# Attention slopes without scaled distance tables, weight splits moved from GpSimd to VectorE, keys made head by head, in a hybrid transformer block

## The chip, the cores and the metric

The kernel runs on one core of a Trainium2 chip. A core has TensorE (PE, matrix products, results in eight PSUM banks), VectorE (DVE), ScalarE (ACT), GpSimd (POOL) and SyncE (SP, which here issues nearly all transfers). The metric is the device time of one execution in microseconds; lower is better.

## The reference

One layer on 512 tokens of width 1024, in float32:

```
h = rms_norm(x); q, k, v, u = split(h @ w_in)          # 4 x 512 columns
a = attention(q, k, v)                                 # 8 heads x 64, causal
    score[t, s] = q[t].k[s] / 8 - slope_h * (t - s);  slope_h = 2 ** -(h + 1), h = 0..7
p = pool(u)       # 4 groups x 128: (trailing mean over 16, 8, 4 or 2 tokens - token) @ w_pool[g] * scale
x = x + concat(a, p) @ w_out
x = x + relu(rms_norm(x) @ w_up) ** 2 @ w_down         # 4096 wide
out = rms_norm(x)
```

The block-sparse selection of the reference takes every past block at this length, so the attention is plain causal attention with a linear distance penalty.

## The kernel before, in words

Every float32 product is made of three matmuls: each factor is split into a high part that PE takes as it is and a low remainder, and `mm3` (lines 193 to 195) adds high x high, high x low and low x high. A split is a cast on ACT and a subtraction, on VectorE or GpSimd, that waits for it (`split_into`, lines 144 and 145). Weights come by DMA into three `raw` buffers (`load`); `prefetch` splits the oldest into `whi` and `wlo` and issues the load of the chunk three further on. The subtraction's engine is the argument `sub`.

The instructions of each engine run in the order in which the program writes them; `in_program_order` fixes that. A stage that is written earlier on one engine therefore holds up what is written behind it on that engine, however ready that is.

The span falls into: normalisation and values (to about 37 us); q0, k0 and u3, the projections of the first pair of heads and of one pooling group; three rounds of the loop at line 554; the output projection in 128-token tiles (`out_tile`), first with the pooling half of w_out, then with the attention half; and the feed-forward part, which is most of the span and which the change doesn't touch.

The heads go in four pairs. A round i of the loop (I call the rounds by the pair whose values they attend: first, second, third pair) does, in program order:

- `pool_mix(g)`: on VectorE the pooled mean minus the token (L505) and a correction of its first 16 columns, where fewer tokens are there to average (L507, L508); then the splits of the mean and of w_pool;
- the projection q of the next pair and its scaled split (`queries`, L387 on ACT, L388 on VectorE), and one weight split;
- the projection u of the next group (`pool_sum`: a copy on ACT, running sums on GpSimd, L498), and two distance tables (`tables`, L369, on GpSimd): the table of token distances `dist`, times the slope of each head;
- `turn`: the probabilities of the pair before are transposed on PE (L455) and split (L459, L461);
- two weight splits; in the third round both have the subtraction on GpSimd;
- the projection k of the next pair and `keys`: for each of two heads, two tiles ka and kb of 128 partitions hold the high half, from ACT, and the low half, from VectorE, in opposite order. Scores take ka first, then kb. Both heads lie in one PSUM bank, on different partitions; where both ACT and VectorE read the bank, the program orders the reads by waits;
- in the third round, between the splits and `keys`, `pool_mix(0)` as well;
- `attend` of the pair (16 matmuls, L473); its result is copied and subtracted (L477 and L478 on ACT, L479 on VectorE, into `cl`), `pool_out` (three matmuls; L519 on ACT, L520 on VectorE), a second `pool_out` and one more weight split in the third round;
- `softmax` of the next pair: 16 score matmuls (L426), for each head in three groups of one bank each, then for each of 8 pieces a minimum with a sum on VectorE (L432: scores, which are negated, plus table, and the smallest), the exponential on ACT (L434) and the scaling on VectorE (L414).

PSUM tiles all come from one rotation of eight banks (`bank`): a new tile waits until the tile eight allocations back has been read.

```
    PART = ((slice(0, 64), slice(64, 128)), (slice(64, 128), slice(0, 64)))
    GROUPS = ((0, 2), (1,), (3,))
```

## Time and profile before

| | |
|---|---|
| runs of before, median of 3 (lowest, highest) | 529.42 us (529.0, 530.33) |
| profiled execution, its own time | 529.51 us |
| its span, first to last instruction | 527.7 us |
| mean granted clock of PE (1 = 2.4 GHz) | 0.992 |
| PE busy | 514.7 us (98%) |
| VectorE busy | 378.9 us (72%) |
| ScalarE busy | 247.8 us (47%) |
| GpSimd busy | 56.0 us (11%) |

Busy shares are means over the whole span. A matmul's duration on the page is longer than its distance to the next one, as matmuls overlap, so a busy PE can hide a lower rate; the granted clock of a stretch and the distance of starts show that. A wait is put down to the instruction that ended last before the waiting one started.

### The profile page before, as it was taken

Reading aid. Unit: us, or ns where it says so; the run is one execution under the profiler, and the core shown is the slowest. Engines: PE = TensorE matmul, PEld = TensorE weight load, DVE = VectorE, ACT = ScalarE, POOL = GpSimd, SP = SyncE. Lnnn points to the kernel's source line nnn. Section 1 sums busy time; section 2 is a strip of 40 time slices with the busy share of each in tenths; the row PEclk is TensorE's granted clock in tenths of the full one; section 3 lists DMA queues with packets and bytes.
Section 4 is the critical chain, followed back from the end, with each engine's and each line's share of the span. In section 5 each row is a group of like instructions: output and inputs, shape, how many; then the busy total and the mean of one; then the engine's idle time right before and its main releaser. Section 6 shows DMA issues by size and latency. Waiting matters only on the chain.

```text
span 527.7 us, 6731 instructions
## 1 busy us (share of the span) xinstructions
PE 514.7 (98%) x2411; PEld 429.4 (81%) x2411; DVE 378.9 (72%) x619; ACT 247.8 (47%) x415; POOL 56.0 (11%) x59
## 2 busy tenths in 40 slices
PE   8999999998999999999999999999999998999995
PEld 5888878886888899888888888888888886888884
DVE  5764898889986756777756777577776778977363
ACT  5534586866744333423323233345655555456033
POOL 2330342516300100000000000000000000000002
PEclk9999999999799999999999999999999999999999
DMA  8441141303224208697777897785688754683012
GB/s 293 146 119 42 49 125 37 126 1 125 81 81 126 74 0 279 202 292 261 260 255 253 251 308 269 250 276 183 218 291 306 273 199 159 223 287 128 0 52 111
DMA packets 74053, 92.48 MB, mean 175 GB/s; under 512 B 4257, under 2 KB 49825, under 8 KB 74018
## 3 DMA queue, kind: packets, MB, share of 16 engines
q1 hardware_dynamic: 73440, 90.98, 52.0%
q10 hardware_dynamic: 578, 1.05, 0.5%
q8 instruction: 19, 0.31, 0.2%
q14 instruction: 16, 0.13, 0.1%
HBM read 75.24 MB, written 16.78 MB: 174 GB/s over the span
## 4 chain that ended last, share of the span: by engine, by line
PE 88%; DVE 6%; ACT 2%; issue 2%; DMA 1%; POOL 0%; SPq 0%; POOLq 0%
PE bank L193 26%; PE bank L195 26%; PE bank L194 26%; PE bank L293 5%; PE bank L426 2%; PE bank L215 1%; DMA wvr<-in_w_in_dram 1%; PE bank L455 1%; DVE ptl L461 1%; DVE p L432 1%; ACT whi L144 1%; DVE wlo L145 1%; DVE ka L398 1%; DVE mx L508 0%; PE bank L473 0%
## 5 line engine op out<-in xcount | busy, mean ns | idle before, releaser
L193 PE MATMUL bank<-hh,whi 128*128 128x512 f32 (+1 forms) x376 | 141.8, 377 | 0.2 <-DVE qs L388 0.2
L195 PE MATMUL bank<-hh,wlo 128*128 128x512 f32 (+1 forms) x376 | 141.4, 376 | 0.0
L194 PE MATMUL bank<-hl,whi 128*128 128x512 f32 (+1 forms) x376 | 141.4, 376 | 0.0
L145 DVE TENSOR_TENSOR wlo<-raw,whi 128x1024 fp32r<-128x1024 f32 x87 | 107.5, 1238 | 27.5 <-ACT whi L144 25.4
L144 ACT CAST whi<-raw 128x1024 fp32r<-128x1024 f32 x90 | 94.1, 1054 | 31.1 <-PE bank L195 23.5
L193 PEld LDWEIGHTS bank<-hh,whi 128*128 128x128 f32 x376 | 70.8, 188 | 13.1 <-PE bank L455 0.4
L195 PEld LDWEIGHTS bank<-hh,wlo 128*128 128x128 f32 x376 | 70.8, 188 | 12.8
L194 PEld LDWEIGHTS bank<-hl,whi 128*128 128x128 f32 x376 | 70.8, 188 | 12.7
L193 PE MATMUL bank<-whi,ah 128*128 128x512 f32 x168 | 65.5, 390 | 0.7 <-DVE a L846 0.7
L194 PE MATMUL bank<-wlo,ah 128*128 128x512 f32 x168 | 65.4, 390 | 0.0
L195 PE MATMUL bank<-whi,al 128*128 128x512 f32 x168 | 65.4, 390 | 0.0
L208 POOL TENSOR_TENSOR rstd<-ms,mhalf 128x1 f32<-128x1 f32 x12 | 6.6, 552 | 388.4 <-DVE ms L203 388.4
L717 DVE TENSOR_TENSOR a<-bank,z 128x512 f32<-128x512 f32 (+1 forms) x31 | 19.7, 636 | 34.2 <-ACT z L711 34.2
L711 ACT ACTIVATE z<-bank 128x512 f32<-128x512 f32 (+1 forms) x35 | 19.6, 560 | 48.9 <-PE bank L195 46.6
L144 ACT CAST ah<-a 128x1024 fp32r<-128x1024 f32 (+1 forms) x28 | 26.3, 941 | 27.9 <-issue 17.8
L145 DVE TENSOR_TENSOR al<-a,ah 128x1024 fp32r<-128x1024 f32 (+1 forms) x28 | 30.5, 1088 | 11.0 <-ACT ah L144 11.0
L193 PEld LDWEIGHTS bank<-whi,ah 128*128 128x128 f32 x168 | 31.5, 188 | 7.6 <-DVE a L846 1.1
L194 PEld LDWEIGHTS bank<-wlo,ah 128*128 128x128 f32 x168 | 31.6, 188 | 6.5
L195 PEld LDWEIGHTS bank<-whi,al 128*128 128x128 f32 x168 | 31.6, 188 | 6.5
L144 ACT CAST rl<-rh 128x512 fp32r<-128x512 f32 x14 | 8.7, 622 | 57.6 <-DVE rh L684 57.6
L199 ACT ACTIVATE sq<-x 128x512 f32<-128x512 f32 (+2 forms) x17 | 10.3, 606 | 33.0 <-DVE x L886 19.6
L434 ACT ACTIVATE p<-p,mn 128x128 f32<-128x128 f32 (+3 forms) x32 | 18.0, 562 | 11.5 <-DVE rs L413 5.8
(149 smaller groups left out, 774.2 us busy)
## 6 DMA issues: line engine op xcount, KB each, us to landing
raw<-in_w_up_dram SPq DMA_DIRECT2D x32, 512.0 KB, 6.3
raw<-in_w_down_dram SPq DMA_DIRECT2D x18, 512.0 KB, 3.3
rh<-in_w_down_dram SPq DMA_DIRECT2D x14, 512.0 KB, 3.3
ta<-rh SPq DMA_DIRECT2D x14, 512.0 KB, 7.3
tb<-rl SPq DMA_DIRECT2D x14, 512.0 KB, 6.6
raw<-in_w_down_dram SPq DMA_DIRECT2D x28, 256.0 KB, 3.4
raw<-in_w_in_dram SPq DMA_DIRECT2D x12, 512.0 KB, 3.8
raw<-in_w_out_dram SPq DMA_DIRECT2D x8, 512.0 KB, 3.2
```

What stands on the lines that cost most here:

```text
L144: nc.scalar.copy(hi, src)
L145: (sub or nc.vector).tensor_sub(lo, src, as32(hi))
L193: nc.tensor.matmul(acc, lhsT=a[0], rhs=b[0], start=first, stop=False)
L194: nc.tensor.matmul(acc, lhsT=a[0], rhs=b[1], start=False, stop=False)
L195: nc.tensor.matmul(acc, lhsT=a[1], rhs=b[0], start=False, stop=last)
L199: nc.scalar.activation(dump, src, AF.Square, scale=1.0 / 32, accum_out=ss[:, k:k + 1])
L208: nc.gpsimd.tensor_tensor(rstd, ms, mhalf, op=ALU.pow)
L293: nc.tensor.matmul(acc, lhsT=a, rhs=w, start=n == 0 and kd == 0, stop=n == 2 and kd == KD - 1)
L426: nc.tensor.matmul(by_qi[qi], lhsT=qs[:, tok(qi)], rhs=k[:, :w], start=n == 0, stop=n == 1)
L434: nc.scalar.activation(p[:, :w], p[:, :w], AF.Exp, scale=-1.0, bias=mn, accum_out=sm)
L711: nc.scalar.activation(z[:, :n * HT], acc, AF.Relu)
L717: nc.vector.tensor_mul(a_p[f // 2][:, at_slots, :], halves(acc), halves(z[:, :n * HT]))
```

## The change

The distance tables are gone. The penalty's slope goes in two places instead: `queries` scales by -0.125 / slope, and the minimum adds the one table `dist` to the scores and multiplies the sum by the slope (`scale` of the same instruction, 1.0 before). `keys` makes both tiles of a head before it begins the next head. All weight subtractions are on VectorE: `cast_next` writes the cast on ACT, and returns a function that writes the subtraction and the next load later. In the first two rounds the first subtraction stands ahead of the keys, as before, and the second behind them; in the third, the first stands inside `pool_mix(0)` between the correction and the splits of the mean, the second behind the keys, and the third, as before, behind the pooling products.

```
+    def cast_next():
+        raw, shape = raws.pop(0)
+        hi = wp.tile([P] + shape, F32R, tag="whi", name="whi")
+        lo = wp.tile([P] + shape, F32R, tag="wlo", name="wlo")
+        nc.scalar.copy(hi, raw)
+        ready.append((hi, lo))
+        def rest():
+            nc.vector.tensor_sub(lo, raw, as32(hi))
+            load()
+        return rest
...
-    def tables(i):
-        tabs = []
-        for j in range(2):
-            tabs.append(at.tile([P, T], F32, tag="tab", name="tab"))
-            nc.gpsimd.tensor_scalar_mul(tabs[j], dist, 2.0 ** (-8.0 * (2 * i + j + 1) / NH))
-        return tabs
...
+    def slope(h):
+        return 2.0 ** (-8.0 * (h + 1) / NH)
...
-    def queries(acc):
+    def queries(acc, i):
         heads = []
-        for m, o in PART:
+        for j, (m, o) in enumerate(PART):
+            scale = -0.125 / slope(2 * i + j)
             qs = at.tile([P, T], F32R, tag="qs", name="qs")
-            nc.scalar.activation(qs[m], acc[m], AF.Copy, scale=-0.125)
-            nc.vector.scalar_tensor_tensor(qs[o], acc[m], -0.125, as32(qs[m]), op0=ALU.mult, op1=ALU.subtract)
+            nc.scalar.activation(qs[m], acc[m], AF.Copy, scale=scale)
+            nc.vector.scalar_tensor_tensor(qs[o], acc[m], scale, as32(qs[m]), op0=ALU.mult, op1=ALU.subtract)
...
         for j, (m, o) in enumerate(PART):
-            heads[j] += [at.tile([P, T], F32R, tag=k, name=k) for k in ("ka", "kb")]
-            nc.scalar.copy(heads[j][1][m], acc[m])
-        for j, (m, o) in enumerate(PART):
-            ka, kb = heads[j][1:]
+            ka, kb = [at.tile([P, T], F32R, tag=k, name=k) for k in ("ka", "kb")]
+            heads[j] += [ka, kb]
+            nc.scalar.copy(ka[m], acc[m])
+            nc.scalar.copy(kb[o], as32(ka[m]))
             nc.vector.tensor_sub(ka[o], acc[m], as32(ka[m]))
-            nc.scalar.copy(kb[o], as32(ka[m]))
-        for j, (m, o) in enumerate(PART):
-            ka, kb = heads[j][1:]
             nc.vector.tensor_copy(kb[m], as32(ka[o]))
...
-                    nc.vector.tensor_tensor_reduce(out=p[:, :w], in0=by_qi[qi], in1=tabs[j][:, T - w:], scale=1.0,
+                    nc.vector.tensor_tensor_reduce(out=p[:, :w], in0=by_qi[qi], in1=dist[:, T - w:],
+                                                   scale=slope(2 * i + j),
                                                    scalar=BIG, op0=ALU.add, op1=ALU.min, accum_out=mn)
...
-    def pool_mix(g, u, s, wpl):
+    def pool_mix(g, u, s, wpl, between=None):
...
+        if between is not None:
+            between()
         split_into(*m_s, mx[:, PAD:])
         split_into(*w_s, wpl)
...
         sums = pool_sum(g - 1, acc)
-        tabs = tables(i + 1)
         pt = [turn(p) for p in probs]
-        prefetch(1, nc.vector if i < NPAIR - 2 else nc.gpsimd)
+        rests = [cast_next(), cast_next()]
         acc = project()
         if i < NPAIR - 2:
-            prefetch(1)
+            rests[0]()
         else:
-            prefetch(1, nc.gpsimd)
-            before, mean = mean, pool_mix(0, *sums)
+            before, mean = mean, pool_mix(0, *sums, rests[0])
         keys(heads, acc)
+        rests[1]()
         fixes = [attend(2 * i + j, pt[j]) for j in range(2)]
         pool_out(g, *(mean if i < NPAIR - 2 else before))
         if i == NPAIR - 2:
             pool_out(0, *mean)
-            prefetch(1, nc.gpsimd)
+            prefetch(1)
```

ScalarE in the first pair's round, from the last weight cast to the copies of the attended values (ka and kb are the key tiles, ch and fix parts of the attended values; the brackets name the engines whose signals an instruction waits for). Before:

```order
L144 CAST whi<-raw 128x1024 [waits DMAHW4_49]
L395 CAST ka<-bank 64x512 [waits PE_49]
L395 CAST ka<-bank 64x512
L399 CAST kb<-ka 64x512 [waits Activation_49] x2
L477 CAST ch_141<-bank 64x512 [waits PE_49]
L478 COPY fix<-bank 64x512
L477 CAST ch_141<-bank 64x512 [waits PE_49]
L478 COPY fix<-bank 64x512
```

In the change, whose lines stand 9 to 19 further down:

```order
L163 CAST whi<-raw 128x1024 [waits DMAHW4_49]
L408 CAST ka<-bank 64x512 [waits PE_49]
L409 CAST kb<-ka 64x512 [waits Activation_49]
L408 CAST ka<-bank 64x512 [waits DVE_49]
L409 CAST kb<-ka 64x512 [waits Activation_49]
L487 CAST ch_141<-bank 64x512 [waits PE_49]
L488 COPY fix<-bank 64x512
L487 CAST ch_141<-bank 64x512 [waits PE_49]
L488 COPY fix<-bank 64x512
```

The first head's second tile now comes ahead of the second head's first tile, and that one has gained a wait for VectorE.

VectorE in the third pair's round, from the end of the pooled mean (mx) to the first minimum of the next softmax (mxl and wpll are the low parts of the mean and of w_pool, wlo the low part of a weight chunk, cl that of the attended and pooled values). Before:

```order
L508 TENSOR_TENSOR mx<-mx,u 128x16 [waits DVE_49]
L145 TENSOR_TENSOR mxl<-mx,mxh 128x512 [waits Activation_49]
L145 TENSOR_TENSOR wpll<-wpl,wplh 128x128 [waits DMAHW6_49,Activation_49]
L398 TENSOR_TENSOR ka<-bank,ka 64x512 [waits PE_49,Activation_49]
L398 TENSOR_TENSOR ka<-bank,ka 64x512
L402 CAST kb<-ka 64x512 [waits DVE_49] x2
L479 TENSOR_TENSOR cl_151<-bank,ch_143 64x512 [waits PE_49,Activation_49] x2
L520 SCALAR_TENSOR_TENSOR cl_154<-bank,psc,ch_146 128x512 [waits Activation_49]
L520 SCALAR_TENSOR_TENSOR cl_153<-bank,psc,ch_145 128x512 [waits Activation_49]
L432 ISA p,mn<-bank,tab 128x128 [waits PE_49,Pool_49]
```

In the change, from behind the correction of mx to just ahead of that minimum:

```order
L167 TENSOR_TENSOR wlo<-raw,whi 128x1024 [waits DMAHW3_49,Activation_49]
L145 TENSOR_TENSOR mxl<-mx,mxh 128x512 [waits Activation_49]
L145 TENSOR_TENSOR wpll<-wpl,wplh 128x128 [waits DMAHW6_49,Activation_49]
L410 TENSOR_TENSOR ka<-bank,ka 64x512 [waits Activation_49]
L411 CAST kb<-ka 64x512 [waits DVE_49]
L410 TENSOR_TENSOR ka<-bank,ka 64x512 [waits Activation_49]
L411 CAST kb<-ka 64x512 [waits DVE_49]
L167 TENSOR_TENSOR wlo<-raw,whi 128x1024 [waits DMAHW4_49]
L489 TENSOR_TENSOR cl_151<-bank,ch_143 64x512 [waits PE_49,Activation_49] x2
L532 SCALAR_TENSOR_TENSOR cl_154<-bank,psc,ch_146 128x512 [waits Activation_49]
L532 SCALAR_TENSOR_TENSOR cl_153<-bank,psc,ch_145 128x512 [waits Activation_49]
L145 TENSOR_TENSOR wlo<-raw,whi 128x1024 [waits DMAHW5_49,Activation_49]
```

Three subtractions wlo have come in, one ahead of mxl, one between the keys and cl, and one ahead of the minimum; the second head's ka waits for ACT anew, and the minimum (no longer shown) waits for PE alone.

## Rows read from the trace of the kernel before

**Rows 1.** The page: busy time of PE, and its slices (40 to the span).

```profile
PE 514.7 (98%) x2411; PEld 429.4 (81%) x2411; DVE 378.9 (72%) x619; ACT 247.8 (47%) x415; POOL 56.0 (11%) x59
...
PE   8999999998999999999999999999999998999995
```

**Rows 2.** Windows: stretch, then busy us (instructions) of each engine, PEclk, DMA share, GB/s.

```profile
99.94:105.78 5.84, 5.84 (x37) 5.22 (x35) 4.47 (x8) 5.32 (x9) 1.91 (x2) 1.00 0.52 182
124.36:136.88 12.52, 9.72 (x40) 7.86 (x39) 10.64 (x17) 8.12 (x16) 4.70 (x3) 0.75 0.24 85
```

**Rows 3.** Waits of PE: line, releaser, us in total, times, longest.

```profile
PE bank L193 <- ACT wplh L144: 1.6, 1, 1.6
PE bank L426 <- DVE kb L402: 1.5, 2, 0.8
...
PE bank L193 <- DVE qs L388: 0.2, 1, 0.2
```

**Rows 4.** Timeline of PE, first pair's scores: start us, us, line, operation.

```profile
77.77 0.22 PE L426 MATMUL bank<-ka,qs 128*128 128x128 f32 x1
78.82 0.30 PE L426 MATMUL bank<-kb,qs 128*128 128x128 f32 x1 [0.83 <-DVE kb L402]
...
81.35 0.40 PE L193 MATMUL bank<-hh,whi 128*128 128x512 f32 x1
```

**Rows 5.** Timeline of PE, third pair: second score matmul, first output-tile matmul.

```profile
132.26 0.45 PE L426 MATMUL bank<-kb,qs 128*128 128x128 f32 x1 [0.68 <-DVE kb L402]
...
136.88 0.63 PE L193 MATMUL bank<-whi,ch 128*128 128x512 f32 x1
```

**Rows 6.** Timeline of VectorE, second pair: correction of the pooled mean.

```profile
89.14 0.17 DVE L507 TENSOR_TENSOR mx<-us,rc 128x16 f32<-128x16 f32 x1
```

**Rows 7.** Timeline of VectorE, third pair: the pooled mean and its split.

```profile
123.05 0.68 DVE L505 SCALAR_TENSOR_TENSOR mx<-us,u 128x512 f32<-128x512 f32 x1
123.65 2.42 DVE L507 TENSOR_TENSOR mx<-us,rc 128x16 f32<-128x16 f32 x1
126.11 2.29 DVE L508 TENSOR_TENSOR mx<-mx,u 128x16 f32<-128x16 f32 x1
129.08 0.69 DVE L145 TENSOR_TENSOR mxl<-mx,mxh 128x512 fp32r<-128x512 f32 x1 [0.68 <-ACT mxh L144]
```

**Rows 8.** Timeline of GpSimd, third pair.

```profile
123.64 4.72 POOL L145 TENSOR_TENSOR wlo<-raw,whi 128x1024 fp32r<-128x1024 f32 x2
```

**Rows 9.** Groups by line (busy us, mean ns of one, idle before it).

```profile
L145 DVE TENSOR_TENSOR wlo<-raw,whi 128x1024 fp32r<-128x1024 f32 x87 | 107.5, 1238 | 27.5 <-ACT whi L144 25.4
L432 DVE CUSTOM_DVE_ANT_0 p<-bank,tab 128x128 f32<-128x128 f32 (+3 forms) x32 | 14.9, 483 | 1.4 <-PE bank L426 1.4
...
L388 DVE SCALAR_TENSOR_TENSOR qs<-bank,qs 64x512 fp32r<-64x512 f32 x8 | 5.5, 688 | 6.6 <-ACT qs L387 6.5
L398 DVE TENSOR_TENSOR ka<-bank,ka 64x512 fp32r<-64x512 f32 x8 | 5.5, 688 | 3.5 <-ACT ka L395 3.4
L479 DVE TENSOR_TENSOR cl<-bank,ch 64x512 fp32r<-64x512 f32 x8 | 5.5, 688 | 2.0 <-ACT fix L478 1.9
...
L402 DVE CAST kb<-ka 64x512 fp32r<-64x512 f32 x8 | 3.4, 419 | 0.1
L520 DVE SCALAR_TENSOR_TENSOR cl<-bank,psc,ch 128x512 fp32r<-128x512 f32 x4 | 2.9, 749 | 0.1
```

**Rows 10.** Timeline of ScalarE, first pair: the two key casts.

```profile
74.74 1.19 ACT L395 CAST ka<-bank 64x512 fp32r<-64x512 f32 x2 [0.41 <-PE bank L195]
```

**Rows 11.** Timelines of VectorE (three rows) and PE (the last), output tiles.

```profile
135.97 0.28 DVE L432 CUSTOM_DVE_ANT_0 p<-bank,tab 128x128 f32<-128x128 f32 x1
...
145.30 1.28 DVE L539 TENSOR_TENSOR x<-bank,x 128x512 f32<-128x512 f32 x2
147.63 1.28 DVE L539 TENSOR_TENSOR x<-bank,x 128x512 f32<-128x512 f32 x2
...
150.12 0.48 PE L193 MATMUL bank<-whi,ch 128*128 128x512 f32 x1
```

More of the change, by code (lines that the diff above doesn't have):

```diff
@@ L393, in keys, with softmax @@
         for j, (m, o) in enumerate(PART):
-            heads[j] += [at.tile([P, T], F32R, tag=k, name=k) for k in ("ka", "kb")]
-            nc.scalar.copy(heads[j][1][m], acc[m])
-        for j, (m, o) in enumerate(PART):
-            ka, kb = heads[j][1:]
+            ka, kb = [at.tile([P, T], F32R, tag=k, name=k) for k in ("ka", "kb")]
+            heads[j] += [ka, kb]
+            nc.scalar.copy(ka[m], acc[m])
+            nc.scalar.copy(kb[o], as32(ka[m]))
             nc.vector.tensor_sub(ka[o], acc[m], as32(ka[m]))
-            nc.scalar.copy(kb[o], as32(ka[m]))
-        for j, (m, o) in enumerate(PART):
-            ka, kb = heads[j][1:]
             nc.vector.tensor_copy(kb[m], as32(ka[o]))
     GROUPS = ((0, 2), (1,), (3,))
-    def softmax(heads, tabs):
+    def softmax(heads, i):
         probs, sums = [[], []], []
@@ L541, in out_tile @@
                 done(half)
-    tabs = tables(0)
-    heads = queries(project())
+    heads = queries(project(), 0)
     prefetch(1)
@@ L551, in hybrid_block @@
     sums = pool_sum(3, acc)
-    probs = softmax(heads, tabs)
+    probs = softmax(heads, 0)
     prefetch(1)
@@ L557, in hybrid_block @@
         acc = project()
-        heads = queries(acc)
+        heads = queries(acc, i + 1)
         prefetch(1)
@@ L575, in hybrid_block @@
             pool_out(0, *mean)
-            prefetch(1, nc.gpsimd)
+            prefetch(1)
         for fix in fixes:
             fix(nc.gpsimd)
-        probs = softmax(heads, tabs)
+        probs = softmax(heads, i + 1)
     wo = [ready.pop(0) for _ in range(4)]
```

## The prediction

> **What bounds the kernel now.** I read the busy table first, then windows over attention, the waits of TensorE (PE), and last the timelines of VectorE (DVE), ScalarE (ACT) and GpSimd (POOL) where PE waits. PE is busy 98% of a span of 527.7 us [rows 1]: time can be won only where PE waits or has half its clock, and a shorter list on another engine is worth nothing by itself. The windows show where that is [rows 2]. Each goes from a pair's first probability-times-value matmul to the first matmul behind its scores; the steps are the same, except that the third pair has one pooling product more. The second pair's stretch lasts 5.84 us at a granted clock of 1.00. The third pair's lasts 12.52 at 0.75, with PE busy for 9.72. The waits name 1.6 us for ACT's split of a pooling weight, 1.5 in two waits for kb, the second key copy, and 0.2 for the queries [rows 3]. By the timelines, one wait for kb stands among the scores of the first pair's round: 1.05 us lie between the starts of two matmuls of 128 columns [rows 4]. The other waits stand in the third pair, where the scores from 132.26 on then take 4.62 us [rows 5]; the first pair's take 2.53 from the same matmul on [rows 4].
>
> The cause is on DVE. The correction of the pooled mean's first 16 columns takes 0.17 us in the second pair [rows 6]. In the third, two such instructions take 2.42 and 2.29 us, and the subtraction of the pooling split follows only at 129.08 [rows 7]. POOL's row tells why: its two weight subtractions run from 123.64 for 4.72 us [rows 8]; the first correction starts 0.01 us later and lasts about as long as one of them, the second as long as the other. Each waited out one POOL subtraction.
>
> **The change part by part.** The profiled execution took 529.51 us, 1.8 more than its span; the median of the runs is 529.42, so a sum against the one holds for the other. Times below are on the clock of before.
>
> *Tables.* Eight multiplications leave POOL. No PE wait names them, so I cost them at nothing; VectorE's first minimum of a softmax no longer waits for POOL.
>
> *Slopes.* The queries are scaled by another constant, the minimum by another than 1.0: the same 8 and 32 instructions. A shorter minimum has no reason. At most the scaling costs a second pass, 14.9 us over four softmaxes [rows 9], or 3.7 each. I take zero, since a multiply-and-subtract of 64x512 takes 688 ns, as a plain subtract does [rows 9].
>
> *Keys head by head, first pair.* The order now has a chain ACT, DVE, ACT, DVE: ACT's cast for the second head waits for VectorE's subtraction of the first. The first cast starts at 74.74 [rows 10] and takes half of 1.19; the subtraction takes 0.69, the copy 0.42 [rows 9]. Head 0 is ready at 76.5, and PE wants it at 77.77 [rows 4]. Head 1 follows at 77.85; PE is there at 79.05. So the 1.05 shrinks to about 0.1, a gain of 0.95. But the later weight split (1.24 [rows 9]) now stands between the keys and the two residuals cl of the attended values (0.69 each), which end at 79.75 and 80.45. The second frees the accumulator bank that PE's next projection takes, at 80.35; with the handover PE waits 0.2. Such a bank wait exists today: the 0.2 for the queries [rows 3]. **First pair: 0.75 won.**
>
> *Second pair.* No score wait is there to win. By the same chain cl is some 0.15 late. **0.15 lost**; PE is then 0.6 early.
>
> *Splits off GpSimd, third pair.* Nothing of POOL lies beside the corrections now. Unhindered, the stretch is 5.84 plus three matmuls of 512 columns (0.7): 6.54 instead of 12.52, so 5.98 is to be won [rows 2], and 0.2 more, since the next matmul's 512 columns still run at half clock (0.63 [rows 5]; 1.2 instead of 2.4 GHz costs them 0.21). Of that the DVE queue keeps a part. DVE is about 0.55 early, so the mean begins at 122.5 instead of 123.05 [rows 7] and the corrections end at 123.5. Then follow, by rows 9: the first weight split to 124.6 (beside ACT's cast of the mean), the two pooling subtractions to 125.5, head 0's keys to 126.6, head 1's (behind ACT's cast) to 127.95, the second split to 129.1, cl to 129.75 and 130.5, and the two residuals of pooling (0.75 each) to 131.25 and 132.0. PE starts the stretch at 123.75 and is free to begin the scores at 127.7, 2.6 us before 130.3, its unhindered end. Both heads are there in time (126.6 for 127.7, 127.95 for 129.0). The banks are not: they go round in eights, and as this stretch allocates one more, head 1's second and third score groups take the banks that the two cl free, and the first output tile the bank that the first pooling residual frees. PE waits until 129.85, 130.6 and 131.35 or so: the stretch ends about 1.1 late. **Third pair: 5.98 - 1.1 + 0.2 = 5.1 won.**
>
> The Trainium skill speaks against this part: Perfetto Trace Analysis, Optimizing Scalar/DVE Operations, says that where VectorE is saturated, offloading some work to GpSimd may make sense (and adds that a shared SBUF read port may spoil it). By its first half, three splits taken back cost VectorE 3 x 1.24 = 3.7 us and return nothing; by the rows, POOL's two held VectorE for 2.42 + 2.29 - 2 x 0.17 = 4.37.
>
> *What is late next.* The last weight split delays the last softmax, which starts near 133.2, against 135.97 before [rows 11], while PE comes 5.5 us earlier. The softmax took 9.3 us before (135.97 to 145.30), with another POOL split beside it, and the add that frees the bank for the third output tile followed 2.3 later [rows 11]. If all 9.3 stay, that bank comes at 145.4; if some 2 of them go with POOL, at 143.4. PE wants it at 144.4 (150.12 - 5.7 [rows 11]). So between 0 and 1.0; I take zero, as nothing of POOL's list but two short adds is left and these end before it. The loads that stand behind the delayed splits on SP's queue come 2 to 3 us later; they run three chunks ahead of the casts, so that costs nothing.
>
> **Sum:** 0.75 - 0.15 + 5.1 = 5.7, and 529.5 - 5.7 = **523.8 us**. From the output tiles on every slice of PE reads 9 up to the 34th of 40, at 435 us [rows 1], so nothing there gives it back. Without the new bank waits (0.2 + 0.15 + 1.1) it is 522.35; with them doubled, 525.25.
>
> **The rivals.**
> 1. *Clock again.* The new waits of the third pair lie within 2 us; the granted clock could fall behind them as it did behind today's. Price: 4.62 - 2.53 + 0.2 = 2.3 us, so 526.1. Against it: the first pair's wait of 0.83 left the following scores at full speed [rows 4].
> 2. *DVE's queue is the bound.* All 3.7 us of the splits land on the path instead of 1.1: 523.8 + 2.6 = 526.4. For it: the bank waits above; against it: the first split lies beside an ACT cast that the next subtraction needs anyway, and the last is wanted only near 134. This is what the skill's offloading rule, in the section named, would make of it.
> 3. *The corrections stay slow,* because POOL was not their cause: keys and residuals 4.37 late, so the wait of 1.1 becomes 5.4 (528.1), and with the clock lost 530.4: no change. Against it: the 0.17 in the second pair, and the start 0.01 us behind POOL's.
> 4. *The scaled minimum is slower.* This is the way to a loss. Each softmax ends up to 3.7 us later; behind each stands the queries' cast, whose bank PE already waits for in the first pair [rows 3], with 0.2 to spare in the second and third and about 0.9 at the output tiles: 3.7 + 3.5 + 3.5 + 2.8 = 13.5, so 537.3. It decides from about 0.22 us more in each of the 32, half of today's mean of 483 ns. Against it: the equal 688 ns [rows 9].
>
> **How the numbers follow.** Forecast 70% (its own range 522.2 to 525.3), rival 1 10%, rival 2 8%, rival 3 7%, rival 4 5%. The range 522.2 to 526.6 holds the forecast and rivals 1 and 2, 88% less what may fall just outside. 0.3%, or 1.6 us, is about what a measurement of this kernel can tell from no change: faster 0.88, same 0.07 (rival 3), slower 0.05 (rival 4).
>
> **What would show it.** Right: the two corrections in the third pair near 0.2 us each; no wait for kb in the first pair; the third stretch at 7.5 to 8 us with clock 1.00; small PE waits before the third pair's last scores and first output tile that name cl; the minimum still near 483 ns. Wrong: a clock below 1.0 there (rival 1), the third stretch above 9 us at full clock (2), corrections still over 1 us (3), PE waits for the queries of over 2 us in every pair (4). A gain above 7.3 us would mean that something outside these stretches moved, which I see no row for.

## The result, and the profile of the changed kernel

The changed kernel takes **524.17 us** (median of 4 runs, 523.5 to 525.57); the kernel before took 529.88 beside it (median of 4, 529.0 to 530.67). The ratio is 0.9896, with a 95% interval of 0.9877 to 0.9916: 1.0% less time, 5.71 us between the medians. The forecast was 523.8.

The profiled execution took 525.57 us, with a span of 523.7. The page, with TensorE's (PE's) busy time, its 40 slices and its granted clock:

```profile
PE 512.3 (98%) x2411; PEld 427.0 (82%) x2411; DVE 374.3 (71%) x622; ACT 248.3 (47%) x415; POOL 36.5 (7%) x48
...
PE   7999999999999999999999999999999998999995
...
PEclk9999999999999999999999999999999999999999
```

PE is still busy for 98% of the span, but that is 2.4 us less busy time than before for the same 2411 matmuls [rows 1]: a matmul at half clock is busy longer (512 columns took 0.63 us at the start of the output tiles [rows 5] and take 0.50 there now). No slice of the clock reads below 9 any more, where before one did:

```profile
PEclk9999999999799999999999999999999999999999
```

The two profiles do not begin alike. The first loads landed later in the changed kernel's (VectorE waits 2.09 us for the first of v's weights, 0.75 before), so its first score matmul starts at 54.40 us instead of 53.00; other profiles below have it anywhere from 52.53 to 54.40. I therefore compare **the body**, from the first score matmul to the last matmul of all, which has nothing of these loads in it. The first and the last of the two, of the kernel before and of the changed one:

```profile
53.00 0.22 PE L426 MATMUL bank<-ka,qs 128*128 128x128 f32 x1
...
521.30 0.28 PE L195 MATMUL bank<-wlh,rl 128*128 128x192 f32 x1
```

```profile
54.40 0.22 PE L435 MATMUL bank<-ka,qs 128*128 128x128 f32 x1
...
517.00 0.28 PE L208 MATMUL bank<-wlh,rl 128*128 128x192 f32 x1
```

The body was 521.30 - 53.00 = 468.30 us and is now 462.60: **5.70 us** less. The windows show where (the same stretches as in [rows 2], from a pair's first probability-times-value matmul to the first matmul behind its scores; the first pair's began at 74.54 and ended at 81.35 before, 6.81 us):

```profile
75.53:81.57 6.04, 6.04 (x36) 5.18 (x35) 4.84 (x8) 5.41 (x9) 0.70 (x1) 1.00 0.34 96
100.26:106.30 6.04, 6.04 (x36) 5.18 (x34) 4.84 (x8) 5.41 (x9) 0.70 (x1) 1.00 0.35 109
124.99:132.66 7.67, 7.18 (x40) 5.70 (x38) 7.25 (x12) 6.81 (x13) 1.41 (x2) 1.00 0.36 114
```

The first stretch went from 6.81 to 6.04, the second from 5.84 to 6.04, the third from 12.52 to 7.67, at a granted clock of 1.00 where it had 0.75. That is 0.77 - 0.20 + 4.85 = 5.42. Another 0.46 comes from ahead of the first pair's round: from the first transpose of the first probabilities to the next projection PE took 2.56 us (66.45 to 69.01) and takes 2.10 (67.85 to 69.95); the 0.2 us wait for the queries [rows 3] is gone. From the third stretch to the attention half of the output projection 13.24 us (136.88 to 150.12) became 13.11 (132.66 to 145.77), 0.13 less, and small differences elsewhere take 0.31 back.

VectorE (DVE) in the third pair, from the pooled mean on, to be held against [rows 7]:

```profile
123.69 0.68 DVE L515 SCALAR_TENSOR_TENSOR mx<-us,u 128x512 f32<-128x512 f32 x1
124.29 0.17 DVE L517 TENSOR_TENSOR mx<-us,rc 128x16 f32<-128x16 f32 x1
124.49 0.18 DVE L518 TENSOR_TENSOR mx<-mx,u 128x16 f32<-128x16 f32 x1
124.58 1.22 DVE L167 TENSOR_TENSOR wlo<-raw,whi 128x1024 fp32r<-128x1024 f32 x1
125.72 0.68 DVE L145 TENSOR_TENSOR mxl<-mx,mxh 128x512 fp32r<-128x512 f32 x1
...
127.97 0.69 DVE L410 TENSOR_TENSOR ka<-bank,ka 64x512 fp32r<-64x512 f32 x1 [0.20 <-ACT ka L408]
...
129.15 1.23 DVE L167 TENSOR_TENSOR wlo<-raw,whi 128x1024 fp32r<-128x1024 f32 x1
130.41 1.41 DVE L489 TENSOR_TENSOR cl<-bank,ch 64x512 fp32r<-64x512 f32 x2
131.85 1.41 DVE L532 SCALAR_TENSOR_TENSOR cl<-bank,psc,ch 128x512 fp32r<-128x512 f32 x2
```

The two corrections take 0.17 and 0.18 us instead of 2.42 and 2.29. The weight splits (124.58 and 129.15) are in the queue now, and the residuals cl of the attended values come behind the second one. What PE waits for there (waits of PE, and the two places in its timeline):

```profile
PE bank L435 <- DVE cl L489: 0.4, 2, 0.2
```

```profile
131.15 0.39 PE L435 MATMUL bank<-ka,qs 128*128 128x256 f32 x1 [0.22 <-DVE cl L489]
...
131.87 0.50 PE L435 MATMUL bank<-ka,qs 128*128 128x512 f32 x1 [0.22 <-DVE cl L489]
```

The wait for wplh (1.6) and those for the keys have gone (1.5 for kb [rows 3], and before also 0.5 for ka, in the third pair); two of 0.2 us for cl are what came in their place, ahead of scores whose bank cl frees.

### The profile page after: what moved, and what is told of

It is laid out like the page before. It is cut to its first block, busy times and chain, and to the rows that moved or that the text cites. A ratio compares the mean times of both kernels' runs of the same rounds, so it can differ in the third digit from the quotient of the medians.

```text
span 523.7 us, 6713 instructions
## 1 busy us (share of the span) xinstructions
PE 512.3 (98%) x2411; PEld 427.0 (82%) x2411; DVE 374.3 (71%) x622; ACT 248.3 (47%) x415; POOL 36.5 (7%) x48
## 3 DMA queue, kind: packets, MB, share of 16 engines
q10 hardware_dynamic: 578, 1.05, 0.5%
## 4 chain that ended last, share of the span: by engine, by line
PE 95%; DMA 1%; DVE 1%; issue 1%; ACT 0%; POOL 0%; SPq 0%; POOLq 0%
PE bank L206 28%; PE bank L207 28%; PE bank L208 28%; PE bank L306 5%; PE bank L483 2%; PE bank L435 2%; PE bank L465 2%; DMA wvr<-in_w_in_dram 1%; PE bank L228 1%; DVE cl L489 0%; DVE a L846 0%; ACT whi L144 0%; POOL o L914 0%; SPq L178 0%; DVE cl L532 0%
## 5 line engine op out<-in xcount | busy, mean ns | idle before, releaser
L145 DVE TENSOR_TENSOR wlo<-raw,whi 128x1024 fp32r<-128x1024 f32 x84 | 103.1, 1228 | 28.1 <-ACT whi L144 25.7
L144 ACT CAST whi<-raw 128x1024 fp32r<-128x1024 f32 x84 | 87.9, 1048 | 31.1 <-PE bank L208 24.2
```

The costliest lines, as they stand in the source:

```text
L144: nc.scalar.copy(hi, src)
L145: (sub or nc.vector).tensor_sub(lo, src, as32(hi))
```

## Experiments

The theory that the forecast rests on: the third pair lost its time because two subtractions on GpSimd (POOL) held VectorE, and the tables and the order of the keys matter little. Its rivals: the tables, the order of the keys, or merely the order of the work in the third round. All times below are medians; "body" is the profile's, from the first score matmul to the last matmul; the stretches are those of the three pairs.

| kernel | us | ratio to before (95%) | body | 1st | 2nd | 3rd |
|---|---|---|---|---|---|---|
| before | 529.29 to 530.39 | | 468.30 | 6.81 | 5.84 | 12.52 |
| the change | 524.17 | 0.9896 (0.9877 to 0.9916) | 462.60 | 6.04 | 6.04 | 7.67 |
| the change, again | 524.31 | 0.9895 (0.9877 to 0.9912) | 462.53 | 6.04 | 6.04 | 7.66 |
| tables dropped only | 528.52 | 0.9977 (0.9965 to 0.9988) | 466.85 | 5.84 | 5.84 | 12.41 |
| keys only | 531.24 | 1.0031 (1.0017 to 1.0046) | 469.83 | 7.48 | 6.57 | 11.78 |
| splits only | 524.86 | 0.9909 (0.9892 to 0.9926) | 463.37 | 6.37 | 6.37 | 7.38 |
| tables dropped and keys | 529.46 | 0.9996 (0.9984 to 1.0007) | 468.29 | 6.20 | 6.21 | 11.43 |
| change, old keys | 525.07 | 0.9916 (0.9900 to 0.9931) | 462.98 | 6.37 | 6.36 | 7.39 |
| change, splits later | 527.76 | 0.9962 (0.9949 to 0.9976) | 465.90 | 5.94 | 5.94 | 7.77 |
| change + 2 subtractions | 529.21 | 0.9993 (0.9978 to 1.0008) | 466.85 | 6.04 | 6.05 | 11.93 |
| change + 6 memsets | 524.32 | 0.9915 (0.9901 to 0.9930) | 462.53 | 6.05 | 6.04 | 7.65 |
| change + 2 multiplications | 526.44 | 0.9955 (0.9938 to 0.9973) | 463.41 | 6.05 | 6.04 | 8.48 |
| winning parts | 523.74 | 0.9892 (0.9873 to 0.9912) | 461.23 | 5.83 | 5.83 | 6.75 |
| winning parts, again | 522.95 | 0.9859 (0.9841 to 0.9876) | 461.28 | 5.84 | 5.84 | 6.76 |

### Each part alone

**Tables dropped only.** The kernel before, with this edit:

```
-        tabs = tables(i + 1)
...
-            nc.scalar.activation(qs[m], acc[m], AF.Copy, scale=-0.125)
+            nc.scalar.activation(qs[m], acc[m], AF.Copy, scale=scale)
...
-                    nc.vector.tensor_tensor_reduce(out=p[:, :w], in0=by_qi[qi], in1=tabs[j][:, T - w:], scale=1.0,
+                    nc.vector.tensor_tensor_reduce(out=p[:, :w], in0=by_qi[qi], in1=dist[:, T - w:],
+                                                   scale=slope(2 * i + j),
```

> The kernel before with one part of the change: no distance tables, slopes in the queries' constant and in the minimum. Keys and splits as before. Theory (the splits on GpSimd are the main cost, the tables cost nearly nothing): GpSimd's two subtractions now begin as soon as the first weight cast ends, near 122.7 us instead of 123.64, still beside the pooled mean and its corrections, so these still lose 3.3 to 4.4 us; the first pair wins up to 0.7 since no table lies beside its two weight splits. Together 0.5 to 1.5 us less than before, about 528.5 to 529.3. Rival (the tables are the gain): 4 to 6 us less, near 524.5. Rival (the scaled minimum or the scaling costs a second pass): slower than before.

Measured: 528.52 us, 0.23% less than before; the body is 1.45 us shorter. The third pair is nearly unchanged, as the theory had it. But the first stretch is 5.84, with no wait in it: this part alone wins all that the first pair had to win, although no key was touched. VectorE's row of before in the first pair:

```profile
73.69 3.20 DVE L145 TENSOR_TENSOR wlo<-raw,whi 128x1024 fp32r<-128x1024 f32 x2
```

GpSimd's of before, the two tables beside it:

```profile
73.63 3.07 POOL L369 TENSOR_SCALAR tab<-dist 128x512 f32<-128x512 f32 x2
```

And VectorE's of this kernel:

```profile
73.12 2.35 DVE L145 TENSOR_TENSOR wlo<-raw,whi 128x1024 fp32r<-128x1024 f32 x2
```

Two weight splits took 3.20 us beside two tables and take 2.35 without. The keys stand right behind them in VectorE's queue. The wait that PE had for kb was the tables' 0.85 us, handed on. In the third pair the pattern moved one instruction forward, as the theory had it. VectorE's mean and corrections there:

```profile
121.92 2.73 DVE L505 SCALAR_TENSOR_TENSOR mx<-us,u 128x512 f32<-128x512 f32 x1
124.58 2.35 DVE L507 TENSOR_TENSOR mx<-us,rc 128x16 f32<-128x16 f32 x1
126.96 0.18 DVE L508 TENSOR_TENSOR mx<-mx,u 128x16 f32<-128x16 f32 x1
```

GpSimd's two weight subtractions beside them:

```profile
121.70 5.19 POOL L145 TENSOR_TENSOR wlo<-raw,whi 128x1024 fp32r<-128x1024 f32 x2 [2.08 <-ACT whi L144]
```

GpSimd's subtractions begin 0.22 us ahead of the mean instead of during it: now the mean takes 2.73 instead of 0.68, and the first correction 2.35. Two instructions wait out two subtractions, whichever two come.

**Keys only.** The kernel before with the new function:

```
-            nc.scalar.copy(heads[j][1][m], acc[m])
-        for j, (m, o) in enumerate(PART):
-            ka, kb = heads[j][1:]
+            nc.scalar.copy(ka[m], acc[m])
+            nc.scalar.copy(kb[o], as32(ka[m]))
             nc.vector.tensor_sub(ka[o], acc[m], as32(ka[m]))
-            nc.scalar.copy(kb[o], as32(ka[m]))
-        for j, (m, o) in enumerate(PART):
-            ka, kb = heads[j][1:]
             nc.vector.tensor_copy(kb[m], as32(ka[o]))
```

> The kernel before with one part of the change: keys made head by head. Tables and splits as before. Theory: the wait for the second key copy goes in the first and third pair, 0.4 to 0.7 us each, and the second pair loses 0.15; the two corrections in the third pair still take 2.3 to 2.4 us each. About 528.9, 1 us less than before. Rival (the order of the keys is the larger part, since the scores wait for it at half clock): 3 us less or more.

Measured: 531.24, **slower** by 0.31% (interval 0.17 to 0.46%). The theory missed here, and so did its rival. The first stretch grew from 6.81 to 7.48, the second from 5.84 to 6.57. ScalarE (ACT) in the first pair shows why:

```profile
78.31 0.58 ACT L396 CAST ka<-bank 64x512 fp32r<-64x512 f32 x1 [1.64 <-DVE ka L398]
```

The second head's cast waits for VectorE's subtraction of the first head, which stands behind the 3.20 us of splits. ACT idles 1.64 us, and the copies of the attended values, which come next in its queue, are that late; cl with them, and PE waits 0.35 and 0.49 us for the banks that cl frees. The third stretch gained 0.74, but from there to the attention half of the output projection it took 13.81 us instead of 13.24 (136.88 to 150.12 before), the first 2.5 of them at a granted clock of 0.67.

**Splits only.** The kernel before with all weight subtractions on VectorE, at the places of the change:

```
-        prefetch(1, nc.vector if i < NPAIR - 2 else nc.gpsimd)
+        rests = [cast_next(), cast_next()]
...
-            prefetch(1, nc.gpsimd)
-            before, mean = mean, pool_mix(0, *sums)
+            before, mean = mean, pool_mix(0, *sums, rests[0])
         keys(heads, acc)
+        rests[1]()
...
-            prefetch(1, nc.gpsimd)
+            prefetch(1)
```

> The kernel before with one part of the change: the three weight subtractions of the third pair on VectorE, at the places of the change. Tables and the old order of the keys kept. Theory: the two corrections in the third pair take about 0.2 us each, the granted clock stays at 1.00 there, and 4 to 5 us of the change's 5.7 come from this part alone: 525 to 526. Rival (GpSimd's work as such is the cause, tables among it): corrections still above 1 us, within 1.5 us of before.

Measured: 524.86, with tables and the old keys still there. The body is 4.93 us shorter, 86% of the change's 5.70, and the third stretch is 7.38 at a granted clock of 1.00. No wait for kb is left, though the keys are made in the old order. The first correction:

```profile
124.53 0.17 DVE L520 TENSOR_TENSOR mx<-us,rc 128x16 f32<-128x16 f32 x1
```

VectorE in the first pair, where one split is left ahead of the keys, beside the first of the two tables:

```profile
74.24 1.63 DVE L167 TENSOR_TENSOR wlo<-raw,whi 128x1024 fp32r<-128x1024 f32 x1
76.52 1.41 DVE L411 TENSOR_TENSOR ka<-bank,ka 64x512 fp32r<-64x512 f32 x2 [0.65 <-ACT ka L408]
```

The table still costs the split some 0.4 us, but VectorE idles 0.65 us behind it, so nothing is handed on to PE.

**The complement: tables dropped and keys, splits as before.** Both edits above, on the kernel before.

> The change without its third part: no tables, keys head by head, but the third pair's three weight subtractions on GpSimd as before. Theory: the corrections in the third pair still lose 3.3 to 4.4 us; the gain is that of the other two parts, 1.2 to 2 us, so about 528.2. Rival (the three parts gain about alike, or the splits only move work from one engine to another): 3 to 4 us less than before, near 526.

Measured: 529.46, ratio 0.9996: **nothing** is left without the splits. The theory had 1.2 to 2 us of gain here and missed, as did its rival. The mean and the first correction take 2.73 and 2.35 again. The stretch itself is 1.09 us shorter than before's, at a granted clock of 1.00 this time, but the clock fell right behind it, in the output tiles:

```profile
123.44:134.87 11.43, 8.22 (x39) 5.68 (x38) 9.18 (x13) 6.98 (x13) 3.67 (x2) 1.00 0.26 93
134.87:137.00 2.13, 2.13 (x6) 1.68 (x7) 2.09 (x9) 1.95 (x6) 1.40 (x1) 0.61 0.01 4
137.00:140.00 3.00, 3.00 (x11) 2.38 (x10) 2.93 (x9) 1.47 (x5) 2.92 (x3) 0.71 0.31 85
```

From there to the attention half of the output projection it took 14.72 us (before: 13.24), which gives 1.48 back. PE was not busy for 3.21 us of the stretch, and the clock's price for that came behind it.

### What it is about GpSimd that holds VectorE

Three kernels put work on GpSimd back into the changed kernel, ahead of the third round's pooled mean. What it writes is read by nothing; everything else is the change's, in the same order.

```
+            for hi, _ in ready[-2:]:
+                echo = at.tile([P, D], F32, tag="echo", name="echo", bufs=1)
+                nc.gpsimd.tensor_sub(echo, x_t[0], as32(hi.rearrange("p a b -> p (a b)") if len(hi.shape) > 2 else hi))
             before, mean = mean, pool_mix(0, *sums, rests[0])
```

> The changed kernel, with two subtractions of 128x1024 added on GpSimd in the third round, where the two of before stood; they read two operands in SBUF and their result is used by nothing. Theory (an instruction of VectorE with two operands in SBUF waits until GpSimd's has ended): the pooled mean and its corrections lose 3.3 to 4.4 us again, the third stretch takes 11 us or more, 528 to 530. Rival (it was the order of the work, not GpSimd's being busy): the corrections stay at 0.2 us each, 524, no difference from the change.

Measured: 529.21, ratio 0.9993: in the time the whole gain is gone, with nothing changed on VectorE. By the body, which is one execution's, 4.25 of the 5.70 us are gone, and 1.45 stay, as much as the tables-only kernel has. VectorE's rows in the third pair:

```profile
123.50 2.77 DVE L515 SCALAR_TENSOR_TENSOR mx<-us,u 128x512 f32<-128x512 f32 x1
126.20 2.40 DVE L517 TENSOR_TENSOR mx<-us,rc 128x16 f32<-128x16 f32 x1
128.64 0.17 DVE L518 TENSOR_TENSOR mx<-mx,u 128x16 f32<-128x16 f32 x1
```

GpSimd's beside them:

```profile
123.29 5.28 POOL L581 TENSOR_TENSOR echo<-x,whi 128x1024 f32<-128x1024 f32 x2 [2.08 <-ACT whi L163]
```

2.77 and 2.40 instead of 0.68 and 0.17: 4.32 us, as much as the 4.37 that the corrections lost before. That is the cause of the third pair's loss, shown by putting it back.

The second replaces the loop by six times `nc.gpsimd.memset(echo, 0.0)`:

> The changed kernel, with six memsets of 128x1024 added on GpSimd in the third round, at the same place; they write SBUF and read nothing, and their result is used by nothing. Theory, by what the Trainium skill states (SBUF - State Buffer, Who interferes with whom: two operands in SBUF put VectorE in the way of GpSimd's reads): corrections stay at 0.2 us each, 524. Rival (any work of GpSimd on SBUF blocks): corrections above 1 us, 526 or more.

Measured: 524.32, no difference from the change. VectorE's mean and first correction, then GpSimd:

```profile
122.47 0.68 DVE L515 SCALAR_TENSOR_TENSOR mx<-us,u 128x512 f32<-128x512 f32 x1
123.07 0.17 DVE L517 TENSOR_TENSOR mx<-us,rc 128x16 f32<-128x16 f32 x1
```

```profile
120.11 6.02 POOL L581 MEMSET echo<- 128x1024 f32 x6
```

GpSimd is busy through the mean and both corrections, and they take 0.68, 0.17 and 0.17 us. The rule of the Trainium skill (SBUF — State Buffer, Who interferes with whom), that a VectorE instruction with two operands in SBUF meets only GpSimd instructions that read SBUF, agrees with this run and the one before.

The third has twice `nc.gpsimd.tensor_scalar_mul(echo, x_t[0], 0.5)`:

> The changed kernel, with two multiplications of 128x1024 by a constant added on GpSimd in the third round, at the same place; one operand is read from SBUF, as the dropped tables did, and the result is used by nothing. Theory (what counts is that GpSimd reads SBUF at all): the mean and its corrections wait for one or both, 2.5 to 6 us more in the third stretch. Rival (one operand leaves room: a weight split of VectorE beside a table took 1.63 us instead of 1.23, not the table's 1.5 more): 0.3 to 1 us more in VectorE's row, at most 1 us in the time.

Measured: 526.44. VectorE's mean, first correction and weight split, then GpSimd:

```profile
122.76 0.68 DVE L515 SCALAR_TENSOR_TENSOR mx<-us,u 128x512 f32<-128x512 f32 x1
123.36 1.01 DVE L517 TENSOR_TENSOR mx<-us,rc 128x16 f32<-128x16 f32 x1
...
124.50 1.22 DVE L167 TENSOR_TENSOR wlo<-raw,whi 128x1024 fp32r<-128x1024 f32 x1
```

```profile
120.43 5.64 POOL L581 TENSOR_SCALAR echo<-x 128x1024 f32<-128x1024 f32 x2
```

Neither expectation holds quite, the rival's row being the nearer. The mean, which begins 2.3 us into the first multiplication (120.43 to 123.2), runs at its usual 0.68, and the split, which begins 1.2 us into the second (from 123.3), at its usual 1.22; only the correction that meets the second one's start takes 1.01 instead of 0.17. So a multiplication of 1024 elements held VectorE for 0.84 us of its 2.8, near its start, and a table of 512 for half of that: two tables added 0.85 to two splits, and in the splits-only kernel one table added 0.41 to one (1.63 against 1.22). The Trainium skill (SBUF — State Buffer, SBUF: two separate sides) says that whichever of the two instructions starts first has the shared ports for the whole of it, and that the other is blocked; with two operands on GpSimd the runs agree (2.09 and 2.23 us lost beside subtractions of 2.4 and 2.8), with one they do not. The stretch grew by 0.8 us and the body by 0.88, the median by some 2 (runs from 525.4 to 527.55; the profiled one was among the shortest). Where the other 1 us lies, this profile does not show.

Which instructions of VectorE are held is not a matter of two operands alone. In the kernel before, GpSimd's third subtraction (136.19 to 138.6) ran beside the last softmax. VectorE there:

```profile
136.18 0.56 DVE L432 CUSTOM_DVE_ANT_0 p<-bank,tab 128x384 f32<-128x384 f32 x1
136.65 0.42 DVE L432 CUSTOM_DVE_ANT_0 p<-bank,tab 128x256 f32<-128x256 f32 x1
137.19 1.48 DVE L414 TENSOR_SCALAR p<-p,rs 128x128 f32<-128x128 f32 x1
```

And the same scaling in the changed kernel, with GpSimd idle:

```profile
136.03 0.29 DVE L423 TENSOR_SCALAR p<-p,rs 128x128 f32<-128x128 f32 x1
```

The minima, which read one operand from PSUM and one from SBUF, ran at their usual 0.56 and 0.42 us; the scaling, which reads its tile and writes it back in SBUF, lost 1.19 us.

### The order of VectorE's queue

**Change with the old keys.** `keys` as before (the diff of keys only, reversed), all else as in the change:

> The changed kernel with one part undone: the keys in the old order (both casts of ScalarE first, then both subtractions, then the copies). No tables and the splits on VectorE stay. Theory formed from the runs of single parts (the wait of the first pair came from the tables beside the weight splits, so head by head has nothing left to win and its chain ACT, DVE, ACT, DVE costs some 0.2 us in each pair): first and second stretch 5.8 to 6.1 us, third 7.4; 0 to 0.8 us less than the change, 523.5 to 524.2. Rival (head by head is a gain once the splits are on VectorE, as the difference between the whole change and the splits alone, 0.7 us, allows): 0.5 to 1 us more than the change, with waits for kb in the first and third pair.

Measured: 525.07, 0.2% above the change, though the intervals overlap; the body is 0.4 longer. The theory missed: the first two stretches are 6.37 and 6.36, not 5.8 to 6.1; the rival was right in sign, but there is no wait for kb. VectorE in the first pair:

```profile
76.22 1.41 DVE L410 TENSOR_TENSOR ka<-bank,ka 64x512 fp32r<-64x512 f32 x2 [1.50 <-ACT ka L407]
```

It idles 1.50 us for ACT's casts of both heads, since only one split stands ahead of the keys, and then has keys, the other split and cl to do in a row. Head by head, a subtraction falls into that idle time (0.90 there in the changed kernel). Together with the other kernels without tables this gives a square, first and second stretch in us:

| | both splits ahead of the keys | one split behind them |
|---|---|---|
| old order of the keys | 5.84, 5.84 | 6.37, 6.36 |
| head by head | 6.20, 6.21 | 6.04, 6.04 |

The two edits only fit each other: each alone costs 0.36 to 0.53 us per pair, both together 0.20. With the tables kept, the first stretch is 6.81 (old order, both splits ahead), 7.48 (head by head, both ahead) and 6.37 (old order, one split behind); the fourth was not run. So with one split behind the keys the first stretch is 6.37 with tables and without. In the third pair the old order is the better one (7.39 against 7.67).

**Splits later.** The changed kernel, with the second subtraction behind the pooling products in every round and the first behind the keys in the third:

```
-            before, mean = mean, pool_mix(0, *sums, rests[0])
+            before, mean = mean, pool_mix(0, *sums)
         keys(heads, acc)
-        rests[1]()
+        if i == NPAIR - 2:
+            rests[0]()
...
         if i == NPAIR - 2:
             pool_out(0, *mean)
+        rests[1]()
```

> The changed kernel with the subtractions moved further back: in the third round the first behind the keys, in all rounds the second behind the pooling products, so that the residuals cl of the attended values, for whose banks PE waits, come first. Theory (the bank waits of the three pairs are VectorE's queue): stretches 5.9, 5.9 and 7.2 instead of 6.07, 6.10 and 7.67; 0.7 to 1 us less than the change. Rival (ScalarE, with its casts of the keys waiting for VectorE's subtractions, is what makes cl late): the stretches stay within 0.1 of the change's, no difference.

Measured: 527.76, 3.6 us **more** than the change; neither expectation had that. The first two stretches did come down to 5.94, but the softmax behind them starts later by a split, and by a long one: here it meets GpSimd's two additions to cl (79.72 to 82.36). VectorE in the first pair:

```profile
81.55 1.90 DVE L167 TENSOR_TENSOR wlo<-raw,whi 128x1024 fp32r<-128x1024 f32 x1
```

The next queries stand behind the softmax (waits of PE):

```profile
PE bank L206 <- DVE qs L400: 2.3, 2, 1.2
```

2.3 us are lost where nothing was lost before. In the third pair one split still stood ahead of cl, the first in the second's place, and VectorE now idles 0.69 us for ACT's cast of the mean, which the first split had filled: the stretch is 7.77, no shorter. What is taken from in front of one waiter lands in front of the next.

**The winning parts together.** Tables dropped; the old order of the keys; in the first two rounds both splits ahead of the keys, as before; in the third round the splits on VectorE, the first inside `pool_mix(0)`, the other two behind the pooling products. On the tables-only kernel:

```
+        if i < NPAIR - 2:
+            prefetch(1)
+        else:
+            rests = [cast_next(), cast_next()]
         acc = project()
         if i < NPAIR - 2:
             prefetch(1)
         else:
-            prefetch(1, nc.gpsimd)
-            before, mean = mean, pool_mix(0, *sums)
+            before, mean = mean, pool_mix(0, *sums, rests[0])
...
             pool_out(0, *mean)
-            prefetch(1, nc.gpsimd)
+            rests[1]()
+            prefetch(1)
```

> A kernel put together from the parts that won: no tables, the old order of the keys, both weight subtractions ahead of the keys in the first two rounds as before; in the third round all three on VectorE, the second and third behind the pooling products. Theory: first and second stretch 5.84 us each, third 6.9 to 7.4; 1 to 1.5 us less than the change, about 523. Rival (the subtractions that are made later delay the last softmax or reach the output tiles too late): the same as the change, or more, with PE waits for wlo or for the residual stream's bank at the output tiles.

> The changed kernel itself, unaltered, beside the kernel put together from the winning parts, on the same chip: 524.2, as measured before. Its own spread (one profile had its first transposed tiles 1.4 us later than that of before, since the first loads landed later) should show as a range of some 2 us.

> The kernel put together from the winning parts once more, beside the changed kernel on the same chip. Theory (from the first scores to the last matmul its profile is 1.37 us shorter than that of the change, 461.23 against 462.60, and this stays in the time): 0.8 to 1.6 us less than the change. Rival (the gain is given back in the feed-forward part, as the medians 523.74 and 524.17 of separate sessions allow): less than 0.5 us between them.

```profile
75.19:81.03 5.84, 5.84 (x37) 5.22 (x35) 4.70 (x8) 5.32 (x9) 1.28 (x1) 1.00 0.62 182
99.62:105.46 5.84, 5.84 (x37) 5.22 (x35) 4.69 (x8) 5.32 (x9) 1.29 (x1) 1.00 0.57 182
124.03:130.79 6.76, 6.71 (x39) 5.74 (x38) 5.94 (x11) 6.61 (x13) 1.89 (x2) 1.00 0.26 80
```

The stretches came out twice at 5.83 to 5.84, as expected, and at 6.75 and 6.76, a little below it; the body is 1.25 to 1.37 us shorter than the change's. The first time the ratio (0.9892) could not be told from the change's 0.9896; side by side on one chip it is 522.95 against 524.31, 0.9859 (0.9841 to 0.9876) against 0.9895 (0.9877 to 0.9912). It is the fastest kernel of this study, 1.1 and 1.4% under the kernel before in its two sessions. PE does not wait for wlo or for the residual stream's bank in it.

## Why the prediction was right, step by step

The total was right: 5.7 us in the sum, 5.70 in the body, 5.71 between the medians. The terms were not all right, and that the sum came out so near is partly luck: the tables' 0.46 was not in it, the third pair gave 0.12 less than its 5.1, and 0.31 went in small differences that it had not either.

- **Tables, "I cost them at nothing": failed.** Dropped alone, they were worth 1.43 us: 0.97 in the first pair (6.81 to 5.84) and 0.46 ahead of it. In the change the 0.46 is theirs; the 0.97 is not theirs alone, since with one split behind the keys they cost the first pair nothing (6.37 with them and without). The step was that no PE wait names them. A wait names the last releaser in the chain, here kb; the tables stood two steps further back, as 3.20 us for two splits that take 1.24 each [rows 9]. The same test of a duration against its group's mean found the third pair's cause; I did not make it in the first. The 0.46 is seen in every kernel without tables (2.10 us from the transposes to the next projection) and in none with them (2.56); the first four scalings of the first softmax, beside GpSimd's running sums, take 3.13 us together in before (the first of them 1.10) and 2.37 in the tables-only kernel (0.29). The sums are GpSimd instructions with two operands, and the first scaling is held beside them as it was beside the subtraction in the last softmax. Why it meets them less without tables is not settled: VectorE's first minimum begins 0.77 us after the first score there and 0.89 in before, which fits a minimum that no longer waits for POOL, but that was not tested apart.
- **Slopes, nothing: right.** The group of the minimum reads as before [rows 9]:

```profile
L441 DVE CUSTOM_DVE_ANT_0 p<-bank,dist 128x128 f32<-128x128 f32 (+3 forms) x32 | 14.9, 483 | 1.1 <-PE bank L435 1.1
```

- **Keys, first pair, 0.75 won: right size, wrong cause.** 0.77 was measured. The parts depend on the order in which they are counted: 0.97 won by dropping the tables and 0.20 given back by the keys and the split behind them; or 0.44 won by the split put behind the keys (6.81 to 6.37), nothing by the tables, and 0.33 by the keys (6.37 to 6.04). The step that the 1.05 shrinks because the heads come one by one was the wrong one: in the old order the wait for kb is gone too, once the tables are dropped or one split stands behind the keys. Keys alone lose, since the chain ACT, DVE, ACT, DVE then runs behind two splits and holds ACT for 1.64. The bank wait of 0.2 and its cause, cl behind the later split, were right.
- **Second pair, 0.15 lost: right** (0.20).
- **Splits, third pair, 5.1 won: right.** 4.85 in the stretch, at full clock, where 4.88 was forecast, and 0.13 of the 0.2 behind it. The estimate of the bare stretch, 6.54, is 0.2 below the shortest that was measured (6.75 and 6.76 in the kernel of the winning parts, with 0.05 us not busy). Over 6.54 VectorE's queue keeps 7.67 - 6.54 = 1.13, the 1.1 of the forecast; over 6.76 it keeps 0.9. Two waits for cl stand where they were put; the third, ahead of the first output tile, the profile names nowhere. The cause is shown by the kernel with the two subtractions put back.
- **Late next, nothing: right.** The last softmax took 7.28 us (134.81 to 142.09) instead of 9.33, with GpSimd's third subtraction gone from beside it, and PE did not wait at the third output tile. The split ahead of it took 1.64 us instead of 1.22, beside the second of GpSimd's two additions (to 133.80).

Of the rivals, the clock (1) did not fall behind waits of 0.2 us; it fell, in or behind the stretch, in each of the four kernels whose mean and corrections again or still lost some 4 us beside GpSimd's subtractions (tables dropped only, keys only, both, and the two subtractions put back). That VectorE's queue would be the bound (2) holds for 7.67 - 6.76 = 0.9 of the 3.7 us of splits, less than the 1.1 forecast and far from all. By the complement, leaving the splits on GpSimd costs 529.46 - 524.17 = 5.3 us. Of the Trainium skill's rule (Perfetto Trace Analysis, Optimizing Scalar/DVE Operations) it is thus the caveat on the shared port that these runs bear out, not the offloading. The corrections staying slow (3) and a slower minimum (4) are refuted by the rows above.

## What to carry to other kernels

When a short instruction takes many times its group's usual duration, look which engine started or ended something at that moment; work moved to an idle GpSimd is not free where VectorE's own instructions beside it read two operands from SBUF, or scale a tile in SBUF. A wait of the bound engine names only the last link, so follow the releaser's own queue back to the first instruction that is longer than its group's mean. Order edits on one queue are not additive (each of two lost 0.4 to 0.5 us per pair, together 0.2), so test them apart and put together what wins.

## What the runs showed of the hardware

- One 128x1024 subtraction on GpSimd, 2.4 to 2.8 us long, held one two-operand instruction of VectorE for 2.05 to 2.25 us, whether that had 16 or 512 elements per partition. It held a one-operand scaling of 128 elements in SBUF for 1.19 us (1.48 against 0.29), and minima of a PSUM and an SBUF operand not at all. Six memsets on GpSimd, 6.02 us, held nothing.
- A one-operand multiplication on GpSimd held VectorE for 0.84 us of 2.8 (1024 elements) or about 0.41 of 1.5 (512), and instructions that began 1.2 and 2.3 us into it ran at their usual 1.22 and 0.68 us.
- The granted clock fell in every kernel in which PE was not busy for 2.0 to 3.2 us of the third stretch, but not always in the same place: 0.75 over the stretch itself, or 1.00 there and 0.61 over the 2.13 us behind it.
